# A decoder layer on one core: four units of the output projection and half the depth of an up-projection unit by a 7-product block scheme

## The chip, the core and the metric

The kernel runs on one core of one Trainium2 chip. The metric is the device time of one launch in microseconds (us). One execution was also taken with the hardware profiler; its rows give the start of each instruction, counted from the start of the span, on TensorE (PE, with its weight loads as PEld), VectorE (DVE), ScalarE (ACT), GpSimd (POOL) and SyncE (SP, which here only issues DMAs).

## What is computed

One layer on 256 tokens of width 2048 (16 chunks of 128), all in f32. Cut to what the change touches:

```python
mix = concat([conv_out, pool_out, att])      # 6 + 6 + 4 chunks of 128
x = x + mix @ w_out                          # 2048 x 2048
h = rmsnorm(x, g_ffn)
u = causal_dwconv(h @ w_up, ffn_conv_w) + ffn_conv_b   # w_up: 2048 x 2*5632
gate, val = split(u, 2)
x = x + (silu(gate) * val) @ w_down
return rmsnorm(x, g_final)
```

## The kernel before

**Precision.** Each f32 product is made of three matmuls in fp32r: both operands are split into a high part `hi` (a copy rounded to fp32r, by ACT) and a low part `lo = raw - hi` (by DVE), and hi·hi, hi·lo and lo·hi are summed in PSUM. The activations (`mixT`, `h2T`, `sums`) are split once, and are the stationary operand (128x128); the weights are split tile by tile as they come, and are the moving operand (128x512).

**The weight stream.** All weights are a list of tiles, `stream`, of 1 MB each (128 partitions x 2048 f32). `next_tile()` takes the next one, and first loads (SP issues the DMA into one of three `raw` buffers) and splits (`split_tile`, L131 on ACT and L132 on DVE) the tiles ahead of it. `raw`, `hi` and `lo` have three buffers each: the `hi` of a tile can start only when PE has ended the tile three places before it. This is the clock of ACT and DVE in all the stages of interest.

**Output projection** (two halves of the columns, 8 tiles each, loop over `n2` ahead of `add_in`). A tile is 2 chunks of depth by 1024 columns: 24 matmuls (`mm_b`, L436, L439, L442: 2 chunks x 2 token blocks x 2 column blocks x 3). The chunks come in the order 6 to 15, then 0 to 5 (`out_order`), since the conv chunks 0 to 5 are made last. After each half `add_in` (L804) adds the four banks of PSUM to `xt` and ACT squares them (L807). In the second half the first 8 chunks of the new x are transposed into `h2T` after tiles 3 and 4 of that half; the other 8 after the first tile of the up-projection.

**Up-projection** (`up`, L845). 11 units of 512 gate and 512 value columns; a unit has 8 tiles of 4 chunks x 512 columns, 24 matmuls each. When a half of a unit is complete, ACT scales it out of PSUM (`z`, L860), and in the middle of the next tile PE transposes it (`pz`, L871) for `up_finish`: the conv, silu and product (L879, L881, L885, L895), whose result goes to `u_raw`.

**Down-projection by blocks** (`turn`, `prod`, `Blocks`). For each pair of units the 1024 rows of `w_down` meet 256 tokens. Split 2 x 2 on depth and on columns (`b11`, `b12`, `b21`, `b22`, 1 MB each, in `ffn`), a 1024-column half is made by 7 products of 12 matmuls (`prod`, L947) where the plain form has 8 times 12. `turn` makes the four sums of the activation blocks (L916 to L918, L921, split by L922 and L925). The sums of the weight blocks are made by DVE (`add`, L245) and by DMAs that add to what is in the buffer, issued by POOL (`add_far`, L242). Each product is added to `xt` by DVE (L953). The 14 products of a pair stand between the up tiles of the next pair, one after each tile. For the first two units no such products are there yet.

**What sets the order.** The instructions of an engine run in the order in which they stand. The framework's scheduler sets it from the order of the code and its own priorities; SP's DMAs wait in one queue, so a load that waits for its buffer holds the loads behind it.

## Time and profile before

| | |
|---|---|
| median of 3 runs (lowest to highest) | 1044.55 us (1044.29 to 1045.07) |
| the profiled execution | 1044.61 us |
| its span, first to last instruction | 1042.7 us |
| DVE busy, ACT busy | 75%, 56% of the span |
| DMA | 220.77 MB, 212 GB/s over the span |
| granted TensorE clock | 0.997 |
| output projection, first and last PE matmul start | 228.4 us and 316.9 us |
| up-projection, first and last PE matmul start | 317.3 us and 983.5 us |

The profiled execution takes 1.9 us more than its span; what is worked out from rows is set against 1044.61 us. A row such as `x1408 | 448.8, 391 | 0.0` gives the count, the busy us, the mean ns of one and the idle us ahead of the group. Matmuls overlap, so the mean of one is longer than its share of the time: shares are read from the chain in order of time, which counts each stretch once.

### The profile page before, as it was taken

The numbers are of one execution on the slowest core, as the hardware profiler recorded it, in microseconds if no ns is written. First come the engines' busy times: TensorE is split into PE (matmuls) and PEld (weight loads), VectorE is DVE, ScalarE is ACT, GpSimd is POOL, SyncE is SP. The second block draws the span as 40 slices with busy tenths as digits, with TensorE's granted clock in tenths as the row PEclk, the third lists the DMA queues.
The fourth block names the chain that finished last, engine by engine and source line by source line (L and its number), as shares of the span: only waits on it lengthen the run. The fifth ranks groups of instructions, "written<-read, shape, count | busy, mean of one in ns | idle before, by whom it ended". The sixth has DMA issues, their size and how long they took to land.

```text
span 1042.7 us, 12612 instructions
## 1 busy us (share of the span) xinstructions
PE 1032.7 (99%) x4994; PEld 867.8 (83%) x4994; DVE 778.2 (75%) x833; ACT 586.7 (56%) x646; POOL 56.6 (5%) x93
## 2 busy tenths in 40 slices
PE   9999999999999999999999999999999999999996
PEld 8888888888888888888888888888888888888885
DVE  5677685764546566978879788797877978789776
ACT  6865354443446545665655655566556655665653
POOL 0013500000000000000000000000000000000000
PEclk9999999999999999999999999999999999999998
DMA  9665465555585464596976979768796687967932
GB/s 328 243 224 180 145 204 190 173 179 184 202 288 197 162 202 145 160 289 194 262 243 167 275 193 261 234 188 258 202 260 222 200 256 206 262 215 195 282 117 81
DMA packets 122020, 220.77 MB, mean 212 GB/s; under 512 B 3906, under 2 KB 35946, under 8 KB 121834
## 3 DMA queue, kind: packets, MB, share of 16 engines
q1 hardware_dynamic: 112426, 201.09, 57.1%
q0 software_dynamic: 9504, 18.88, 11.3%
q8 instruction: 39, 0.64, 0.2%
q14 instruction: 19, 0.16, 0.0%
q10 hardware_dynamic: 32, 0.01, 0.0%
HBM read 217.86 MB, written 2.10 MB: 211 GB/s over the span
## 4 chain that ended last, share of the span: by engine, by line
PE 98%; DVE 1%; ACT 0%; issue 0%; DVEq 0%
PE pu L845 46%; PE pp_a L947 9%; PE pp_b L947 5%; PE po L442 3%; PE po L439 3%; PE po L436 3%; PE pp_c L947 2%; PE pa_cb L403 2%; PE pa_pv L403 2%; PE pa_cx L403 2%; PE pa_cc L403 2%; PE pp L966 2%; PE pz L871 2%; PE pk L493 1%; PE pa_q L403 1%; PE pa_cb L407 1%
## 5 line engine op out<-in xcount | busy, mean ns | idle before, releaser
L845 PE MATMUL pu<-hi,h2T 128*128 128x512 f32 x1408 | 448.8, 391 | 0.0
L132 DVE TENSOR_TENSOR lo<-raw,hi 128x2048 fp32r<-128x2048 f32 (+3 forms) x156 | 333.0, 2136 | 137.8 <-ACT hi L131 137.2
L131 ACT ACTIVATE hi<-raw 128x2048 fp32r<-128x2048 f32 (+3 forms) x156 | 279.4, 1794 | 154.3 <-PE po L442 39.2
L845 PEld LDWEIGHTS pu<-hi,h2T 128*128 128x128 f32 x1408 | 264.4, 188 | 54.2
L845 PE MATMUL pu<-lo,h2T 128*128 128x512 f32 x704 | 274.6, 390 | 0.0
L253 DVE TENSOR_TENSOR lo<-ffn,hi 128x2048 fp32r<-128x2048 f32 x63 | 144.2, 2290 | 66.6 <-ACT hi L252 66.6
L252 ACT ACTIVATE hi<-ffn 128x2048 fp32r<-128x2048 f32 x63 | 120.7, 1917 | 98.0 <-PE pu L845 73.7
L845 PEld LDWEIGHTS pu<-lo,h2T 128*128 128x128 f32 x704 | 132.3, 188 | 27.5 <-DVE lo L132 0.7
L947 PE MATMUL pp_a<-hi,sums 128*128 128x512 f32 x288 | 94.5, 389 | 0.0
L881 DVE SCALAR_TENSOR_TENSOR t<-pz,cols,t 128x255 f32<-128x255 f32 (+1 forms) x176 | 79.5, 478 | 10.2 <-ACT t L879 9.2
L879 ACT ACTIVATE t<-pz,cols 128x256 f32<-128x256 f32 x88 | 46.9, 558 | 46.2 <-DVE t L881 24.1
L947 PEld LDWEIGHTS pp_a<-hi,sums 128*128 128x128 f32 x288 | 54.1, 188 | 11.2
L242 POOL DMA_DIRECT2D ffn<-in_w_down_dram x18 | 23.2, 1291 | 615.3 <-DVE ffn L245 494.3
L860 ACT ACTIVATE z<-pu,r_x 128x512 f32<-128x512 f32 x44 | 30.2, 687 | 46.7 <-PE pu L845 46.7
L947 PE MATMUL pp_a<-lo,sums 128*128 128x512 f32 x144 | 56.1, 389 | 0.0
L947 PE MATMUL pp_b<-hi,sums 128*128 128x512 f32 x144 | 47.3, 389 | 0.0
L245 DVE TENSOR_TENSOR ffn<-ffn 128x2048 f32<-128x2048 f32 x18 | 41.2, 2286 | 0.0
L436 PE MATMUL po<-hi,mixT 128*128 128x512 f32 x128 | 39.6, 391 | 0.0
L442 PE MATMUL po<-hi,mixT 128*128 128x512 f32 x128 | 39.5, 389 | 0.0
L439 PE MATMUL po<-lo,mixT 128*128 128x512 f32 x128 | 39.4, 389 | 0.0
L947 PEld LDWEIGHTS pp_a<-lo,sums 128*128 128x128 f32 x144 | 27.0, 188 | 5.6
L947 PEld LDWEIGHTS pp_b<-hi,sums 128*128 128x128 f32 x144 | 27.0, 188 | 5.6
(223 smaller groups left out, 1287.1 us busy)
## 6 DMA issues: line engine op xcount, KB each, us to landing
raw<-in_w_up_dram SPq DMA_DIRECT2D x88, 1024.0 KB, 7.3
ffn<-in_w_down_dram SPq DMA_DIRECT2D x40, 1024.0 KB, 6.2
raw<-in_w_in_dram SPq DMA_DIRECT2D x28, 1024.0 KB, 5.0
ffn<-in_w_down_dram POOLq DMA_DIRECT2D x18, 1024.0 KB, 10.4
raw<-in_w_out_dram SPq DMA_DIRECT2D x16, 1024.0 KB, 4.9
raw<-in_w_kv_dram SPq DMA_DIRECT2D x4, 1024.0 KB, 6.9
raw<-in_w_down_dram SPq DMA_DIRECT2D x4, 1024.0 KB, 5.2
raw<-in_w_kv_dram SPq DMA_DIRECT2D x6, 512.0 KB, 8.4
```

What stands on the lines that cost most here:

```text
L131: nc.scalar.activation(hi[:, s, :], raw[:, s, :], AF.Copy)
L132: nc.vector.tensor_tensor(lo[:, s, :], raw[:, s, :], hi[:, s, :].bitcast(F32), op=ALU.subtract)
L252: nc.scalar.activation(hi, raw, AF.Copy)
L253: nc.vector.tensor_tensor(lo, raw, hi.bitcast(F32), op=ALU.subtract)
L403: nc.tensor.matmul(ps[mi], hi[:, kk, c], actT[:, k, :], start=first and kk == 0, stop=False)
L436: nc.tensor.matmul(ps[tb][n], ah, hi[:, kk, c], start=f, stop=False)
L439: nc.tensor.matmul(ps[tb][n], ah, lo[:, kk, c], start=False, stop=False)
L442: nc.tensor.matmul(ps[tb][n], al, hi[:, kk, c], start=False, stop=l)
L845: nc.tensor.matmul(ps[tb], x_, y_[:, kk, :], start=k == 0 and n == 0, stop=k == KC - 1 and n == 2,)
L879: nc.scalar.activation(t, v, AF.Identity, bias=cvec("ffn_conv_b", m), scale=cw[2])
L881: nc.vector.scalar_tensor_tensor(t[:, s:], v[:, : S - s], cw[2 - s], t[:, s:], op0=ALU.mult, op1=ALU.add)
L947: nc.tensor.matmul(ps, a, b[:, j, :], start=first and j == 0 and n == 0, stop=j == 3 and n == 2, skip_group_check=True,)
```

## The change

Two more places use the 7-product scheme.

**Output projection.** Chunks 6 to 13 (8 chunks, "four units" of two) by the right 1024 columns are done by 7 products, `p0` to `p6`, in place of four tiles. The 12 tiles that stay are called `t0` to `t11` here: t0 to t7 are the first half, t8 to t11 the rest of the second. The order on PE is t0 t1 t2 t3 t4 p0 t5 p1 t6 p2 t7 p3 p4 t8 p5 t9 p6 t10 t11. The activation sums are made at the start of the stage from `mixT` (hi and lo are added again, L933, then `make_forms`, L887 to L899) and stored in the upper half of `h2T`; the blocks of `w_out` and the raw sums are in a new tile `outp`, which takes the buffer that `hT` had.

**Up-projection, unit 1.** Units 0 and 1 are run together. The tiles of unit 0 are called `u0` to `u7`. Unit 1 (gate and value columns together, 1024) is done for chunks 0 to 7 by 7 products, `m0` to `m6`, and for chunks 8 to 15 by four tiles, `v12`, `v13` (gate) and `v02`, `v03` (value), so called after the pair in `UP_ORDER`. The order is u0 to u4, m0, u5, m1, u6, m2, u7, m3, v12, v13, m4, v02, m5, v03, m6. Here the partial sums of several products share a bank, and what one result must not have of the bank's sum is copied out (`snaps`, L1037 to L1041) and taken off again when the half is scaled out (`z`, L1064 to L1068: three on DVE, one on ACT, where before all were on ACT).

The first blocks of `w_down`, which were loaded ahead of unit 0, are now loaded when unit 1's products are being split. In the code behind, `turn` calls `make_forms`, which has the same instructions.

```diff
@@ -202,10 +202,6 @@
     out_order = list(range(NCONV, KC)) + list(range(NCONV))
-    for n2 in range(2):
-        for k in out_order[::2]:
-            plan_b(w_out, k, 2, n2 * 1024, 1024, 2)
@@ -220,19 +216,25 @@
-        def __init__(self, seq, gi, p):
-            self.seq, self.gi, self.p = seq, gi, p
-            self.k0 = group_of[gi][0] * 4
+        def __init__(self, seq, gi, p, w=w_down):
+            self.seq, self.gi, self.p, self.w = seq, gi, p, w
+            self.k0 = NCONV if gi is None else group_of[gi][0] * 4
@@ -281,6 +283,35 @@
+    class OutBlocks(Blocks):
+        def buf(self, name):
+            return out_raw[:, {"b11": 0, "b22": 1, "b12": 2, "b21": 2}[name]]
+        def stationary(self, i, j):
+            if 1 <= i <= 4:
+                return out_form[:, i - 1, 0, j], out_form[:, i - 1, 1, j]
+            tb, s = {0: (0, 0), 5: (0, 1), 6: (1, 1)}[i]
+            k = NCONV + 2 * j + s
+            return tuple(mixT[:, k, h * S + tb * P : h * S + (tb + 1) * P] for h in range(2))
+    out_blocks = OutBlocks(0, None, 1, w_out)
+    out_sched = []
+    for n2 in range(2):
+        pairs = out_order[::2] if n2 == 0 else out_order[8::2]
+        for i, k in enumerate(pairs):
+            out_sched.append((n2, k, i == 0, i == len(pairs) - 1))
+            n_after = ((0, 0, 0, 0, 1, 1, 1, 2), (1, 1, 0, 0))[n2][i]
+            for _ in range(n_after):
+                out_sched.append(("prod", sum(o[0] == "prod" for o in out_sched)))
+    for o in out_sched:
+        if o[0] == "prod":
+            stream.append((out_blocks, None, o[1], 1))
+        else:
+            plan_b(w_out, o[1], 2, o[0] * 1024, 1024, 2)
@@ -294,6 +325,31 @@
+    class UpBlocks(Blocks):
+        U = 1
+        def source(self, name):
+            s, h = int(name[1]) - 1, int(name[2]) - 1
+            c0 = (1 - h) * D_UP + self.U * 512
+            src = w_up[: 8 * P, c0 : c0 + 512]
...
+    up_blocks = UpBlocks(2, None, 0)
+    up_blocks.next = blocks[0]
+    UP_ORDER = [0, 1, 2, 3, 4, ("m", 0), 5, ("m", 1), 6, ("m", 2), 7, ("m", 3), ("m", (1, 2))]
+    UP_ORDER += [("m", o) for o in ((1, 3), 4, (0, 2), 5, (0, 3), 6)]
@@ -307,6 +363,11 @@
         for t in range(n_t):
+            if gi == 0:
+                if t == 0:
+                    for o in UP_ORDER:
+                        sched.append(("up", 0, o) if isinstance(o, int) else ("mixed", UpBlocks.U, o[1]))
+                continue
             sched.append(("up", a + t // 8, t % 8))
             for _ in range(after[t]):
                 sched.append(prods.pop(0))
@@ -319,6 +380,10 @@
+        elif what == "mixed" and isinstance(b, int):
+            stream.append((up_blocks, None, b, 1))
+        elif what == "mixed":
+            plan_b(w_up, 4 * b[1], 4, (1 - b[0]) * D_UP + a * 512, 512, 4)
         else:
             stream.append((a, None, b, 1))
@@ -809,21 +874,92 @@
-    for n2 in range(2):
-        ps = [[bank(f"po_{n2}_{tb}_{n}") for n in range(2)] for tb in range(TB)]
-        for i in range(KC // 2):
-            mm_b(ps, next_tile(), mixT, out_order[2 * i : 2 * i + 2], range(TB), i == 0, i == KC // 2 - 1)
-            if n2 == 1 and i in (2, 3):
-                transpose_in(xt, h2T, "g_ffn", range((i - 2) * 4, (i - 1) * 4), "x2")
-        add_in(ps, n2 * 2, range(TB), f"o{n2}", ssq4)
+    def make_forms(raw, form, four, own, nm, t=None):
+        v = raw.rearrange("p (j s) (b t) -> p s b j t", s=2, b=TB)
+        a11, a12, a21, a22 = v[:, 0, 0], v[:, 1, 0], v[:, 0, 1], v[:, 1, 1]
+        if t is None:
+            t = wpool.tile([P, 4, 4, P], F32, tag="raw", name=f"turn_{nm}")
...
+        tt(t[:, 0], a21, a22, op=ALU.subtract)
+        tt(t[:, 2], a11, a21, op=ALU.subtract)
+        tt(t[:, 1], t[:, 0], a11, op=ALU.subtract)
+        tt(t[:, 3], t[:, 1], a12, op=ALU.add)
+        nc.scalar.activation(four(0), t, AF.Copy)
+        tt(four(1), t, four(0).bitcast(F32), op=ALU.subtract)
+    outp = apool.tile([P, 4, 2048], F32, tag="act", name="outp")
+    out_raw = outp[:, :3, :].rearrange("p i (j c) -> p i j c", c=512)
+    mix_raw = outp[:, 3, :].rearrange("p (c t) -> p c t", t=S)
+    mix_8 = mixT[:, NCONV : NCONV + 8, :].bitcast(F32)
+    nc.vector.tensor_tensor(mix_raw, mix_8[:, :, :S], mix_8[:, :, S:], op=ALU.add)
+    out_form = h2T[:, 8:, :].rearrange("p (f s) (j t) -> p f s j t", s=2, t=P)
+    make_forms(
+        mix_raw, None, lambda half: out_form[:, :, half], (), "mix",
+        out_blocks.buf("b12").rearrange("p j (f t) -> p j f t", t=P),
+    )
+    at_tile = 0
...
+        n2, k, first, last = o
+        if first:
+            ps = [[bank(f"po_{n2}_{tb}_{n}") for n in range(2)] for tb in range(TB)]
+            at_tile = 0
+        mm_b(ps, next_tile(), mixT, (k, k + 1), range(TB), first, last)
+        at_tile += 1
+        if n2 == 0 and at_tile <= 3:
+            out_blocks.load(("b11", "b22", "b12")[at_tile - 1])
+        if n2 == 1 and at_tile in (2, 3):
+            transpose_in(xt, h2T, "g_ffn", range((at_tile - 2) * 4, (at_tile - 1) * 4), "x2")
+        if last:
+            add_in(ps, n2 * 2, range(TB), f"o{n2}", ssq4)
-    for name in ("b11", "b22", "b12"):
-        blocks[0].load(name)
@@ -852,12 +988,84 @@
+        if u == 0 and b == 1:
+            h2_8 = h2T[:, :8, :].bitcast(F32)
+            nc.vector.tensor_tensor(u_raw, h2_8[:, :, :S], h2_8[:, :, S:], op=ALU.add)
+            make_forms(
+                u_raw, None, lambda half: sums[:, 1:5, half], (), "h2",
+                up_blocks.buf("b12").rearrange("p j (f t) -> p j f t", t=P),
+            )
+            for name in ("b11", "b22", "b12"):
+                up_blocks.load(name)
+        todo.append(lambda: up_finish(u, w, z))
+    def up_mixed(u, what):
+        hi, lo = next_tile()
+        r = r_2[0]
+        snaps = [u_raw[:, 4 + 2 * i : 6 + 2 * i, :].rearrange("p c t -> p (c t)") for i in range(2)]
+        if what == 1:
+            up_ps["snap"] = wpool.tile([P, 512], F32, tag="raw", name="snap")
+        snaps.append(up_ps.get("snap"))
...
+        if isinstance(what, int):
+            chain, first = (("a", 1), ("b", 1), ("a", 0), ("a", 0), ("b", 0), ("c", 0), ("a", 0))[what]
+            ps = mm(
+                chain, [up_blocks.stationary(what, j) for j in range(4)], bool(first), what != 5
+            )
+            if what in (0, 2):
+                nc.scalar.activation(snaps[what // 2], ps, AF.Copy, scale=r[:, 0:1])
+            elif what == 1:
+                nc.scalar.activation(snaps[2], ps, AF.Copy, scale=r[:, 1:2])
+            elif what == 3:
+                nc.vector.scalar_tensor_tensor(
+                    snaps[2], ps, r[:, 1:2], snaps[2], op0=ALU.mult, op1=ALU.subtract
...
+                chain = ("c", "a")[tb] if not right else ("b", "d")[tb]
+                mm(chain, pairs, q == 2 and chain in "cd", q == 3)
...
+        z = [spool.tile([P, 512], F32, tag="w2k", name=f"z_{u}_{w}_{tb}") for tb in range(TB)]
+        stt = nc.vector.scalar_tensor_tensor
+        if w == 0:
+            stt(z[0], up_ps["b"], r[:, 0:1], snaps[1], op0=ALU.mult, op1=ALU.subtract)
+            stt(z[1], up_ps["d"], r[:, 1:2], snaps[2], op0=ALU.mult, op1=ALU.subtract)
+        else:
+            stt(z[0], up_ps["c"], r[:, 0:1], snaps[0], op0=ALU.mult, op1=ALU.add)
+            nc.scalar.activation(z[1], up_ps["a"], AF.Copy, scale=r[:, 1:2])
         todo.append(lambda: up_finish(u, w, z))
@@ -1072,7 +1233,7 @@
     for what, a, b in sched:
-        {"up": up, "prod": prod, "plain": plain}[what](a, b)
+        {"up": up, "mixed": up_mixed, "prod": prod, "plain": plain}[what](a, b)
```

How the built programs differ at the three places that the prediction speaks of. Line numbers of the changed kernel are its own.

The first place is DVE at the end of the input projection and the start of the output projection. Before, the queue reads as follows; lo_2217, lo_2284 and lo_2314 are the low parts of the second, third and fourth tile of `w_out` (t1, t2 and t3 in the names above):

```order
L132 TENSOR_TENSOR lo_2217<-raw_2176,hi_2216 128x2048
L778 SCALAR_TENSOR_TENSOR cv_2160<-cu_2154,cols,cv_2160 128x256
L778 SCALAR_TENSOR_TENSOR cv_2170<-cu_2164,cols,cv_2170 128x256
L778 SCALAR_TENSOR_TENSOR cv_2160<-cu_2154,cols,cv_2160 128x256
L778 SCALAR_TENSOR_TENSOR cv_2170<-cu_2164,cols,cv_2170 128x256
L132 TENSOR_TENSOR lo_2284<-raw_2214,hi_2283 128x2048
L537 TENSOR_TENSOR mixT<-pat_2252,mixT 128x256
L421 TENSOR_TENSOR cb_2261<-pa_cb_0_2174,cb_2261 128x256
L421 TENSOR_TENSOR cb_2268<-pa_cb_1_2175,cb_2268 128x256
L422 TENSOR_TENSOR cb_2261<-cb_2261,row_x 128x256
```

After, at the same place, lo_2217 is again t1's (t2's, lo_2292, stands two rows behind the end of this piece):

```order
L933 TENSOR_TENSOR outp<-mixT 128x2048
L602 TENSOR_TENSOR mixT<-pat_2252,mixT 128x256
L486 TENSOR_TENSOR cb_2261<-pa_cb_0_2174,cb_2261 128x256
L486 TENSOR_TENSOR cb_2268<-pa_cb_1_2175,cb_2268 128x256
L487 TENSOR_TENSOR cb_2261<-cb_2261,row_x 128x256
L487 TENSOR_TENSOR cb_2268<-cb_2268,row_x 128x256
L855 TENSOR_TENSOR cb_2261<-cb_2261,cv_2160 128x256
L855 TENSOR_TENSOR cb_2268<-cb_2268,cv_2170 128x256
L890 TENSOR_TENSOR outp<-outp 128x512
L602 TENSOR_TENSOR mixT<-cb_2261,mixT 128x256
L602 TENSOR_TENSOR mixT<-cb_2268,mixT 128x256
L891 TENSOR_TENSOR outp<-outp 128x512
```

The rebuilding of the raw activations (L933) stands where t2's low part stood, the three small sums stand between the conv's last steps, and t2's low part is behind all of them.

The second place is DVE and SP in the up-projection's first tiles. Before, on DVE, from the last transposes into `h2T` on, the low parts of u3, u4, u5 and u6 follow each other:

```order
L346 SCALAR_TENSOR_TENSOR h2T<-pt_x_12_2880,cols,h2T 128x256 x2
L346 SCALAR_TENSOR_TENSOR h2T<-pt_x_14_2889,cols,h2T 128x256 x2
L132 TENSOR_TENSOR lo_2913<-raw_2832,hi_2912 128x2048
L132 TENSOR_TENSOR lo_2945<-raw_2910,hi_2944 128x2048
L132 TENSOR_TENSOR lo_2975<-raw_2942,hi_2974 128x2048
L132 TENSOR_TENSOR lo_3005<-raw_2972,hi_3004 128x2048
```

After, lo_2928 and lo_2968 are u3's and u4's, lo_2998 is m0's and lo_3028 is u5's:

```order
L411 SCALAR_TENSOR_TENSOR h2T<-pt_x_14_2904,cols,h2T 128x256 x2
L132 TENSOR_TENSOR lo_2928<-raw_2847,hi_2927 128x2048
L891 TENSOR_TENSOR ffn<-ffn 128x512
L892 TENSOR_TENSOR ffn<-ffn 128x512
L895 TENSOR_TENSOR ffn<-ffn 128x512
L132 TENSOR_TENSOR lo_2968<-raw_2925,hi_2967 128x2048
L899 TENSOR_TENSOR sums<-ffn,sums 128x4x512
L255 TENSOR_TENSOR lo_2998<-ffn,hi_2997 128x2048
L247 TENSOR_TENSOR ffn<-ffn 128x2048
L132 TENSOR_TENSOR lo_3028<-raw_2995,hi_3027 128x2048
```

On SP, after, raw_2995, raw_3055 and raw_3108 are the loads of u5, u6 and u7, and the next row is the load of block b12 of `w_up` (the loads of b11 and b22 stand further ahead); before, loads of up tiles follow each other here:

```order
L120 DMA raw_2995<-in_w_up_dram 128x4x512
L120 DMA raw_3055<-in_w_up_dram 128x4x512
L120 DMA raw_3108<-in_w_up_dram 128x4x512
L241 DMA ffn<-in_w_up_dram 128x4x512
L120 DMA raw_3187<-in_w_up_dram 128x4x512
```

Block b12's buffer holds the raw sums until L899 has read them, so its load comes after L899; DVE's add of b12 to b11 (L247) waits for that load, and u5's low part (lo_3028) stands right behind the add.

The third place is DVE where the first half of unit 1 is scaled out. Before, that is ACT's work (ACT's queue, L860, the gate half of unit 1):

```order
L131 ACTIVATE hi_3254<-raw_3222 128x2048
L131 ACTIVATE hi_3284<-raw_3252 128x2048
L860 ACTIVATE z_0_0_3312<-pu_0_0_3160,r_x_2901 128x512
L860 ACTIVATE z_0_1_3314<-pu_0_1_3161,r_x_2901 128x512
L131 ACTIVATE hi_3320<-raw_3282 128x2048
L879 ACTIVATE t_0_0_3346<-pz_0_0_3336,cols 128x256
```

After, on DVE, lo_3322 is v02's low part, lo_3352 is m5's and lo_3373 is v03's:

```order
L132 TENSOR_TENSOR lo_3322<-raw_3259,hi_3321 128x2048
L1089 SCALAR_TENSOR_TENSOR t_1_3_3300<-pz_1_2_3283,cols,t_1_3_3300 128x255
L1089 SCALAR_TENSOR_TENSOR t_1_3_3300<-pz_1_2_3283,cols,t_1_3_3300 128x254
L1103 TENSOR_TENSOR ffn<-t_0_3_3170,t_1_3_3300 128x256
L255 TENSOR_TENSOR lo_3352<-ffn,hi_3351 128x2048
L1064 SCALAR_TENSOR_TENSOR z_0_0_3368<-pm_b,r_x_2916,ffn 128x512
L1065 SCALAR_TENSOR_TENSOR z_0_1_3369<-pm_d,r_x_2916,snap 128x512
L132 TENSOR_TENSOR lo_3373<-raw_3349,hi_3372 128x2048
L1089 SCALAR_TENSOR_TENSOR t_0_0_3399<-pz_0_0_3389,cols,t_0_0_3399 128x255
L1089 SCALAR_TENSOR_TENSOR t_0_0_3399<-pz_0_0_3389,cols,t_0_0_3399 128x254
```

The two scalings (L1064, L1065) have moved from ACT to DVE, and stand behind m5's low part.

More of the change, by code (lines that the diff above doesn't have):

```diff
@@ new lines, with prod @@
+    chains = {}
+    def prod(bl, i):
+        hi, lo = next_tile()
+        chain, first, tb, right, op = (
+            ("a", True, 0, 0, ALU.add),
+            ("b", True, 1, 1, ALU.add),
+            ("a", False, 0, 1, ALU.subtract),
+            ("a", False, 1, 1, ALU.subtract),
+            ("b", False, 0, 1, ALU.add),
+            ("c", True, 0, 0, ALU.add),
+            ("a", False, 1, 0, ALU.add),
+        )[i]
+        if first:
+            chains[chain] = bank(f"pp_{bl.gi}_{bl.p}_{chain}")
+        ps = chains[chain]
+        for j in range(4):
+            ah, al = bl.stationary(i, j)
+            for n, (a, b) in enumerate(((ah, hi), (ah, lo), (al, hi))):
+                nc.tensor.matmul(
+                    ps, a, b[:, j, :], start=first and j == 0 and n == 0,
+                    stop=j == 3 and n == 2, skip_group_check=True,
+                )
+        c0 = bl.p * 1024 + right * 512
+        o = xt[:, tb, c0 : c0 + 512]
+        nc.vector.tensor_tensor(o, o, ps, op=op)
```

105 lines of the change are left out of this document (58 added, 47 removed).

## The prediction

> **What bounds the kernel now.** The page's first part and its chain of waits (shares of the span) come first, then the chain in order of time (start, us, what):
>
> ```profile
> PE 1032.7 (99%) x4994; PEld 867.8 (83%) x4994; DVE 778.2 (75%) x833; ACT 586.7 (56%) x646; POOL 56.6 (5%) x93
> PE 98%; DVE 1%; ACT 0%; issue 0%; DVEq 0%
> ```
> ```profile
> 317.43 5.45 PE pu L845 x24
> 322.88 1.75 PE pt_x L334 x16
> 354.57 0.87 PE pz L871 x8
> 431.60 2.72 PE pp_a L947 x12
> 443.39 5.44 PE pu L845 x24
> ```
>
> The path to the end is TensorE's row of matmuls, one behind the other. A tile of 24 takes 5.44 us, a product of 12 takes 2.72: 0.2267 us each. What an engine beside PE does counts only where PE waits for it. The view of the up-projection's line shows how seldom it does (us, times):
>
> ```profile
>   DVE lo L132: 0.7, 3
> ```
>
> So the question is in two parts: what leaves PE's row, and where the added work of DVE, ACT and the DMAs comes too late.
>
> **What leaves the row.** Output projection: four tiles (96 matmuls) become seven products (84). Unit 1's first 8 chunks: the same, 96 to 84. Transposes stay as many. That is 24 matmuls x 0.2267 = **5.44 us**, 2.72 in each place. How one matmul is priced is a choice; the groups by line give two other figures for it (busy us, mean ns of one, idle ahead):
>
> ```profile
> L845 PE MATMUL pu<-hi,h2T 128*128 128x512 f32 x1408 | 448.8, 391 | 0.0
> L845 PEld LDWEIGHTS pu<-hi,h2T 128*128 128x128 f32 x1408 | 264.4, 188 | 54.2
> ```
>
> 391 ns is the length of one with its overlap; 24 of these would make 9.4 us, and the tile takes 5.44, so it is no price. 188 ns is its weight load, with 54.2 us of idle time between the loads: loads are not back to back. I take the tile's 0.2267. The Trainium skill, "Perfetto Trace Analysis", section "Identifying the Most-Contended Engine", says that matmul busy time is no measure of how close TensorE is to its limit, and that the share of weight loads is to be used. On the first the trace agrees (391 ns against 227). By the second the 24 would be worth their weight loads, 24 x 0.188 = 4.51 us, an estimate; the tile of 24 taking 5.44 us, not 4.51, speaks against it.
>
> **What is added to DVE and ACT, in sum.** The windows (us, then busy and count of PE, PEld, DVE, ACT, POOL; clock; DMA share; GB/s) of the output projection, of units 0 and 1, and of a stage that has the 7-product scheme already:
>
> ```profile
> 228.40:316.90 88.50, 88.50 (x401) 73.47 (x400) 45.94 (x39) 36.75 (x37) 0.00 (x0) 1.00 0.64 224
> 317.40:405.00 87.60, 87.60 (x409) 73.06 (x408) 50.94 (x56) 49.66 (x61) 0.96 (x5) 1.00 0.56 185
> 430.00:560.00 130.00, 130.00 (x592) 107.97 (x591) 107.87 (x97) 76.31 (x68) 6.00 (x5) 1.00 0.78 227
> ```
>
> The durations of what is added are there, since later stages run the same forms. In order of time on DVE, a large sum, an addition to xt and an add of two blocks; then the group rows of a small sum and of the only scaling from PSUM with 512 columns:
>
> ```profile
> 429.71 2.29 DVE L925 TENSOR_TENSOR sums<-turn,sums 128x2048 fp32r<-128x2048 f32 x1
> 431.91 2.29 DVE L132 TENSOR_TENSOR lo<-raw,hi 128x2048 fp32r<-128x2048 f32 x1
> ...
> 436.38 0.68 DVE L953 TENSOR_TENSOR xt<-xt,pp_a 128x512 f32<-128x512 f32 x1
> 436.97 2.29 DVE L245 TENSOR_TENSOR ffn<-ffn 128x2048 f32<-128x2048 f32 x1
> 439.18 2.28 DVE L132 TENSOR_TENSOR lo<-raw,hi 128x2048 fp32r<-128x2048 f32 x1
> ```
> ```profile
> L917 DVE TENSOR_TENSOR turn<-ffn x5: 678/685/686, 420.2 to 936.4; 128x512 f32<-128x512 f32 x5
> L578 DVE SCALAR_TENSOR_TENSOR misc<-pv,r_mem,misc x2: 730/735/740, 71.5 to 72.1; 128x512 fp32r<-128x512 f32 x2
> ```
>
> From start to start a 128x2048 takes 2.21 us (429.71 to 431.91), a 128x512 0.59, a scaling about 0.65. The output projection gets 3 more low parts (19 tiles for 16), two block adds, L933 and L899 (8 x 2.21 = 17.7), 4 small sums (2.4) and 7 additions to xt (4.1): 24.2, hence 70 of 85.8 us, 82%. Units 0 and 1 get the same without the seven additions, and four scalings: 50.9 + 17.7 + 2.4 + 2.6 = 73.6 of 84.9, 87%. The stage at 430 has 83% with PE busy all of its 130 us. So DVE stays below PE; the small excess over the known 83% is a reason to follow the queue where it is tight. ACT gets four copies (about 1.9 each) and stays under 60 us. No cost can be below nothing here: PE is busy all of both windows, so there is no idle time to win. Each block scheme also loads 6 MB for 4: some 2 MB more in each stage, to about 250 GB/s, against a stage that had 227 with the same scheme.
>
> **Where it is tight: three places of DVE's queue, and one more.** The clock of hi and lo is read from ACT and DVE (start, us, engine, line; in brackets idle time and what ended it), beside PE's first matmul of the stage:
>
> ```profile
> 227.45 0.40 PE L407 MATMUL pa_cb<-hT,lo 128*128 128x256 f32 x2
> 228.41 0.63 PE L436 MATMUL po<-hi,mixT 128*128 128x512 f32 x2
> ```
> ```profile
> 245.00 1.92 ACT L131 ACTIVATE hi<-raw 128x2048 fp32r<-128x2048 f32 x1 [3.52 <-PE po L442]
> ```
> ```profile
> 226.24 1.66 DVE L778 SCALAR_TENSOR_TENSOR cv<-cu,cols,cv 128x256 f32<-128x256 f32 x4
> 232.20 0.75 DVE L421 TENSOR_TENSOR cb<-pa_cb,cb 128x256 f32<-128x256 f32 x2
> 232.86 0.75 DVE L422 TENSOR_TENSOR cb<-cb,row_x 128x256 f32<-128x256 f32 x2
> 246.95 2.29 DVE L132 TENSOR_TENSOR lo<-raw,hi 128x2048 fp32r<-128x2048 f32 x1 [3.15 <-ACT hi L131]
> 298.98 1.65 DVE L346 SCALAR_TENSOR_TENSOR h2T<-pt_x,cols,h2T 128x256 fp32r<-128x256 f32 x4
> 324.23 3.23 DVE L346 SCALAR_TENSOR_TENSOR h2T<-pt_x,cols,h2T 128x256 fp32r<-128x256 f32 x8 [1.25 <-PE pt_x L334]
> ```
>
> The third tile ends at 228.41 + 3 x 5.44 = 244.73; its buffer's next hi starts 0.27 later, the low part 1.95 behind and is done 2.21 on: 4.43 us from buffer to split tile.
>
> *Start of the output projection.* L933 writes into hT's old buffer, which PE reads until about 227.8; DVE is busy to 227.9 anyway. Behind it stand 2.2 (L933), 7 steps of 256 columns (two take 0.66, so 2.35), a small sum (0.6), 2 such steps (0.7), two sums (1.2) and t2's low part (2.2): done at 237.1 to 237.6. PE wants t2 at 228.41 + 10.88 = 239.29. Margin 1.7 or more; cost 0. Even twice the price for L933 would cost 0.5.
>
> *From t7 to t8.* t8's hi waits for t7's end, t8's low part is ready 4.43 after it, and p3 and p4 keep PE for 5.44. Margin 1.0; cost 0.
>
> *Block b12 of unit 1.* Up tiles now start 2.72 earlier, at 314.71. u1's low part waits for t10's buffers (6.3 before that), so it ends at 312.8; the four steps of the last transposes (1.65) and `add_in` (2.4) end at 316.9. Then come u2's low part, L993, a small sum, the eight steps (3.2), u3's low part, three small sums, u4's low part and L899: 2.2 x 5 + 0.6 x 4 + 3.2 + some 0.5 for the rstd = 17.1, to 334.0. Only then can b12's load be issued. The loads of such blocks (view of their line, 280 to 560 us; then the page's rows of issues, median us to landing last):
>
> ```profile
> DMA to landing us min/median/max: 6.0/6.2/9.9
> ```
> ```profile
> ffn<-in_w_down_dram SPq DMA_DIRECT2D x40, 1024.0 KB, 6.2
> ffn<-in_w_down_dram POOLq DMA_DIRECT2D x18, 1024.0 KB, 10.4
> ```
>
> With 6.2 it lands at 340.2, the add ends at 342.4, u5's low part at 344.6. PE wants u5 after u0 (5.45), the transposes (1.75), u1 to u4 (21.76) and m0 (2.72): 346.39. Margin 1.8, less about 0.5 for hand-overs: a landing of up to some 7.5 us costs nothing. At 9.9 it costs 2.4, at POOL's 10.4 2.9. I take 0, since the load of u7 is the only one right ahead of it; bounds 0 to 2.9. Behind the waiting add stand the low parts of u5 and m1, and PE waits for them. The loads that add (POOL) have about 9 us to spare: b12's sum is needed only for p3 and m3.
>
> *Scaling of unit 1's gate half.* Say m4 ends at T. m5's hi waits for v13's buffer, free at T - 2.72; its low part runs from T - 0.5 to T + 1.7. The two scalings stand behind it: T + 2.35 and T + 3.0. PE transposes both in the middle of v02, the second from T + 2.83. It waits **about 0.3 us**. Before, ACT did this. Bounds: 0, if the scalings run as fast as an addition to xt, to 0.9, if the low part is another 0.6 late. m6's half has one scaling on each engine and a whole tile of time: 0.
>
> **The sum.** 1044.61 - 5.44 + 0.3 = 1039.5 us. The profiled execution (1044.61) stands 0.06 over the median of the runs (1044.55), which is less than their spread of 0.8; no correction.
>
> **Rivals.**
>
> *Block b12 comes late* (chance 13%). For it: b12 is behind L899 in a queue that I followed by hand over 17 us, and one of the eleven loads of its kind took 9.9 us. Against: the median of 6.2 with two adding DMAs about. Price 1 to 2.9 us: 1040.5 to 1042.4; most of this is still faster.
>
> *Many small waits* (6%): each of the 14 new products waits 0.15 to 0.3 us, as the three waits of 0.7 in all show that margins near 0 do exist. 2.1 to 4.2 us: 1041.6 to 1043.7. Against: the products from 430 to 560 stand in the same alternation, and PE is busy all of that window.
>
> *A matmul is worth its weight load* (3%): 1044.61 - 4.51 + 0.3 = 1040.4. This is the skill's rule above.
>
> *DVE becomes the bound: slower than before* (7%). If the new operations, which read mixT and h2T in strided pieces and write into the halves of h2T and sums, cost a multiple, DVE's sum passes PE's. In the output projection this begins where the added 24.2 become 39.9 (1.65 times), and the layer is slower than before by 0.2% from about 47 us on, or, with both stages over, from some 43.5 and 37.6. From there it is 1046.7 and more; between the two points the time is about that of before. Against: L917 and L925 read and write such pieces already, at 0.59 and 2.21 from start to start.
>
> That the work isn't removed is no rival: the order of PE holds 24 matmuls fewer.
>
> **How the numbers follow.** The forecast has 71%, and by itself 1038.8 (the lowest run of before less 5.44, and no wait) to 1040.4. The range reaches into the first two rivals, **1038.7 to 1042.0**; beyond it lie the end of the late landing, most of the small waits, and DVE as the bound. A measurement of this kernel can tell 0.2%, 2.1 us, from no change: faster means under 1042.46, slower over 1046.6. Faster: 71 for the forecast, 12 of the 13 for b12, 2 of the 6 for small waits, 3 for the weight loads, 88 in all. Same: 1 of b12, 4 of the small waits, 2 of DVE as the bound, 7. Slower: the other 5 of DVE.
>
> **What would show it.** PE should have 24 matmuls fewer, and the chain should be all but PE. Out of the projection: PE's first up matmul at 314.7 instead of 317.4; if later, the missing part has its row among PE's waits, for t2, t8 or a product. In units 0 and 1: a wait of pz for DVE's z of 0.2 to 0.4 us at some 389 us; none at u5 near 346; if there is one, DVE's L247 should show idle time that ended with a DMA. First product of w_down at about 426.5 (431.6 before). I am wrong if PE's row has idle time over 1 us in all between 228 and 430, or if a matmul in the new tiles starts at another spacing than 0.227 us.

## The result, and the profile after

| | median of runs (lowest to highest) | ratio to before, 95% interval |
|---|---|---|
| before | 1044.59 us (1044.29 to 1045.07) | |
| after | 1039.19 us (1038.98 to 1039.66) | 0.9948 [0.9936, 0.996] |

The kernel became 5.40 us faster, within the forecast's own range and 0.3 us under its 1039.5. The profiled execution took 1039.66 us, with a span of 1037.9.

The page of the changed kernel, busy times and shares of the chain:

```profile
PE 1026.7 (99%) x4970; PEld 861.9 (83%) x4970; DVE 820.5 (79%) x866; ACT 601.8 (58%) x654; POOL 64.1 (6%) x97
PE 98%; DMA 1%; DVE 0%; SPq 0%; DVEq 0%; issue 0%; ACT 0%
```

PE has 24 matmuls fewer (4994 to 4970), and is still what bounds the kernel; DVE went from 75% to 79%. The view of PE's waits between 228 and 430 us has no row, before or after. The chain in order of time (start, us, what) of the changed kernel gives the stages; in front of it stands the first matmul of the output projection, from the timeline:

```profile
228.90 0.63 PE L501 MATMUL po<-hi,mixT 128*128 128x512 f32 x2
```
```profile
315.20 5.45 PE pu L981 x24
...
344.17 2.72 PE pm_a L1024 x12
346.89 5.44 PE pu L981 x24
...
386.77 2.73 PE pm_c L1024 x12
389.50 0.22 PE pz L1079 x2
389.72 0.24 PE pm_a L1024
389.96 0.67 PE pz L1079 x6
390.63 2.51 PE pm_a L1024 x11
...
426.68 2.72 PE pp_a L921 x12
```

In this execution the output projection began 0.49 us later than in the one of before (228.90 to 228.41), ahead of anything that was changed; so lengths are compared, not times of day.

| stretch | before | after | difference |
|---|---|---|---|
| t0 to u0 | 317.43 - 228.41 = 89.02 | 315.20 - 228.90 = 86.30 | -2.72 |
| u0 to the first product of `w_down` | 431.60 - 317.43 = 114.17 | 426.68 - 315.20 = 111.48 | -2.69 |

Each place gave back its 12 matmuls (2.72), and all waits together cost 0.03 us. A new product takes 2.72 like the old ones. The windows of the two stretches (us, then busy of PE, PEld, DVE, ACT, POOL):

```profile
228.40:314.00 85.60, 85.60 (x390) 71.14 (x389) 66.12 (x54) 44.78 (x41) 2.74 (x2) 1.00 0.77 245
314.70:399.00 84.30, 84.30 (x394) 70.23 (x393) 69.41 (x71) 56.27 (x64) 5.87 (x7) 1.00 0.70 210
```

DVE is at 77% and 82%, PE is busy all of both, and the DMAs move 245 and 210 GB/s.

### The profile page after: what moved, and what is told of

Its sections match the earlier page's. It is cut to its first block, busy times and chain, and to the rows that moved or that the text cites. A ratio compares the mean times of both kernels' runs of the same rounds, so it can differ in the third digit from the quotient of the medians.

```text
span 1037.9 us, 12624 instructions
## 1 busy us (share of the span) xinstructions
PE 1026.7 (99%) x4970; PEld 861.9 (83%) x4970; DVE 820.5 (79%) x866; ACT 601.8 (58%) x654; POOL 64.1 (6%) x97
## 4 chain that ended last, share of the span: by engine, by line
PE 98%; DMA 1%; DVE 0%; SPq 0%; DVEq 0%; issue 0%; ACT 0%
PE pu L981 42%; PE pp_a L921 9%; PE pp_b L921 5%; PE pp_c L921 2%; PE pa_cb L468 2%; PE pa_pv L468 2%; PE pa_cx L468 2%; PE pa_cc L468 2%; PE po L504 2%; PE pp L1127 2%; PE po L501 2%; PE po L507 2%; PE pz L1079 2%; PE pm_a L1024 2%; PE pa_q L468 1%; PE pk L558 1%
## 5 line engine op out<-in xcount | busy, mean ns | idle before, releaser
L981 PE MATMUL pu<-hi,h2T 128*128 128x512 f32 x1280 | 409.4, 391 | 0.0
L132 DVE TENSOR_TENSOR lo<-raw,hi 128x2048 fp32r<-128x2048 f32 (+3 forms) x148 | 314.7, 2128 | 70.9 <-ACT hi L131 69.9
L131 ACT ACTIVATE hi<-raw 128x2048 fp32r<-128x2048 f32 (+3 forms) x148 | 264.3, 1789 | 110.5 <-issue 34.7
L981 PEld LDWEIGHTS pu<-hi,h2T 128*128 128x128 f32 x1280 | 240.3, 188 | 49.4
L981 PE MATMUL pu<-lo,h2T 128*128 128x512 f32 x640 | 249.5, 390 | 0.0
L255 DVE TENSOR_TENSOR lo<-ffn,hi 128x2048 fp32r<-128x2048 f32 x70 | 160.3, 2290 | 72.0 <-ACT hi L254 72.0
L254 ACT ACTIVATE hi<-ffn 128x2048 fp32r<-128x2048 f32 x70 | 134.0, 1916 | 105.1 <-PE pu L981 75.0
L1087 ACT ACTIVATE t<-pz,cols 128x256 f32<-128x256 f32 x88 | 46.9, 558 | 48.1 <-DVE t L1089 24.2
L247 DVE TENSOR_TENSOR ffn<-ffn 128x2048 f32<-128x2048 f32 x20 | 45.7, 2287 | 3.4 <-DMA ffn<-in_w_up_dram 3.4
L468 PE MATMUL pa_cb<-hT,hi 128*128 128x512 f32 x96 | 30.7, 400 | 0.0
L468 PE MATMUL pa_pv<-hT,hi 128*128 128x512 f32 x96 | 30.2, 396 | 0.0
L468 PE MATMUL pa_cc<-hT,hi 128*128 128x512 f32 x96 | 30.2, 395 | 0.0
```

The costliest lines, as they stand in the source:

```text
L131: nc.scalar.activation(hi[:, s, :], raw[:, s, :], AF.Copy)
L132: nc.vector.tensor_tensor(lo[:, s, :], raw[:, s, :], hi[:, s, :].bitcast(F32), op=ALU.subtract)
L247: nc.vector.tensor_tensor(self.buf(to), self.buf(to), self.buf(what), op=ALU.add)
L254: nc.scalar.activation(hi, raw, AF.Copy)
L255: nc.vector.tensor_tensor(lo, raw, hi.bitcast(F32), op=ALU.subtract)
L468: nc.tensor.matmul(ps[mi], hi[:, kk, c], actT[:, k, :], start=first and kk == 0, stop=False)
```

## The experiments

The theory: the gain is 24 x 0.2267 us out of PE's row, the parts add up, and all else is hidden by margins of about 1 us. Against it stand a price by weight loads, and an end that something else sets (a late block, DVE). Each edit is made in the changed kernel, and each time is set against its 1039.19 us and, as a ratio, against runs of before on the same chip. Line numbers move by a few between kernels.

### The two halves apart

*Output projection alone*: units 0 and 1 in their old order, `forms` and the loads of their blocks left out, the loads of `w_down` ahead of unit 0 again.

```diff
-            if gi == 0:
-                if t == 0:
-                    for o in UP_ORDER:
...
-        if u == 0 and b == 1:
...
+    for name in ("b11", "b22", "b12"):
+        blocks[0].load(name)
```

> Only the output projection has the block scheme; units 0 and 1 of the up-projection are as before. If TensorE's row is the bound and each of the 12 matmuls that leave it is worth 0.2267 us: 2.72 us less than before, 1041.9 us, with PE's first up matmul 2.72 us earlier after the start of the projection than before, and no wait of PE in that stage. If a matmul is worth its weight load of 188 ns: 2.26 less, 1042.3. If the whole gain comes from the up-projection: no change, 1044.6. If the gain of the full change were more than its parts (DVE relieved elsewhere), less than 2 us here.

*Units 0 and 1 alone*: the output projection as before.

```diff
-        pairs = out_order[::2] if n2 == 0 else out_order[8::2]
+        pairs = out_order[::2]
...
+            n_after = 0
...
-    make_forms(
-        mix_raw, None, lambda half: out_form[:, :, half], (), "mix",
...
```

> Only unit 1's first 8 chunks have the block scheme; the output projection is as before. TensorE's row as the bound: 2.72 us less than before, 1041.9 us, so that the two halves add up to the full change's 5.4. By weight loads: 1042.3. If the new waits (block b12, the scalings on DVE) cost here what was left open (0.3 and up to 2.9 us), 1042.2 to 1044.8.

Measured: 1041.94 us (0.9976 [0.9967, 0.9986]) and 1041.88 us (0.9973 [0.9962, 0.9983]), each against its 1044.61. That is -2.67 and -2.73; their sum, -5.40, is what both did together. The chains of the two, first u0, then the first product of `w_down`:

```profile
316.47 5.45 PE pu L978 x24
...
430.65 2.72 PE pp_a L916 x12
```
```profile
317.10 5.45 PE pu L968 x24
...
428.61 2.72 PE pp_a L921 x12
```

From u0 to the first product it is 114.18 us with the old units (114.17 before) and 111.51 with the new (111.48 after). The profiled execution of the first kernel took 1043.55 us, 1.6 more than its median, and began the projection late, at 230.17 us; from there to u0 it is 86.30, the length of the changed kernel. The 5.4 us come from these two places, half each, and neither costs the other anything.

### What a matmul is worth

The seven products of the output projection with each matmul cut into two of 256 columns: the same columns through PE, twice the weight loads in 84 matmuls.

```diff
+            parts = (slice(0, 256), slice(256, 512)) if bl is out_blocks else (slice(0, 512),)
...
-                nc.tensor.matmul(ps, a, b[:, j, :], ...)
+                for c in parts:
+                    nc.tensor.matmul(ps[:, c], a, b[:, j, c], ...)
```

> In the seven products of the output projection each matmul of 512 columns is made as two of 256, so 24 matmuls and 24 weight loads a product in place of 12; the same sums. If a matmul costs its columns (256-column matmuls of the input projection start 0.12 us apart): a product takes 24 x 0.12 = 2.88 for 2.72 us, 7 of them 1.1 us more than the changed kernel, some 1040.3. If the weight load of 0.188 us is what paces TensorE: 24 x 0.188 = 4.5 us a product, 12.5 us more, 1051.7.

Measured: 1040.42 us (0.9961 [0.9946, 0.9977]), +1.2. In the chain of this kernel, a product of 24 halves, and in its groups by line, their weight loads (busy us, mean ns of one, idle ahead):

```profile
263.86 2.87 PE pp_None_b L923 x24
```
```profile
L923 PEld LDWEIGHTS pp_None_b<-hi,h2T 128*128 128x128 f32 x32 | 4.6, 192 | 0.1
```

The product takes 2.87 us in place of 2.72, so a half starts every 0.12 us, while one weight load is 0.192 us long: loads overlap, and the mean length of a load is no price any more than that of a matmul is. Seven products at 0.15 more are 1.05 of the 1.2 us. The Trainium skill, "Perfetto Trace Analysis", section "Identifying the Most-Contended Engine", takes the share of weight loads, beside the share of the peak FLOPs, as what tells how near TensorE is to its limit. That a matmul is worth its weight load was the prediction's reading of it, and is not borne out here: 84 loads more cost 1.2 us, and 24 matmuls fewer saved 5.40.

### A block that comes late

The load of b12 of unit 1 is issued twice, so that the block lands some 5 us later.

```diff
-            for name in ("b11", "b22", "b12"):
+            for name in ("b11", "b22", "b12", "b12"):
                 up_blocks.load(name)
```

> Block b12 of unit 1 is loaded twice, the second load into the same place behind the first, so that its sum waits for the second. In the profile of the changed kernel the load lands 5.5 us after its issue, DVE's add waits 3.4 us for it, and u5's low part is ready at 345.75, 1.1 us before PE wants it. If that margin is what hides the wait: the second load lands 2.5 to 5.5 us later, and the kernel takes 1.4 to 4.4 us more than the changed one, 1040.6 to 1043.6, with PE waiting for u5's low part. If the wait of DVE is off the path whatever its length: 1039.2, no change.

Measured: 1040.17 us (0.9954 [0.9941, 0.9968]), +1.0: less than the theory of the margin gives (1.4 to 4.4). DVE's timeline (start, us; in brackets the idle time ahead and what ended it) of the changed kernel, then of this one, shows why:

```profile
335.59 2.28 DVE L255 TENSOR_TENSOR lo<-ffn,hi 128x2048 fp32r<-128x2048 f32 x1
341.25 2.29 DVE L247 TENSOR_TENSOR ffn<-ffn 128x2048 f32<-128x2048 f32 x1 [3.38 <-DMA ffn<-in_w_up_dram]
343.46 2.29 DVE L132 TENSOR_TENSOR lo<-raw,hi 128x2048 fp32r<-128x2048 f32 x1
```
```profile
335.12 2.28 DVE L255 TENSOR_TENSOR lo<-ffn,hi 128x2048 fp32r<-128x2048 f32 x1
340.30 2.29 DVE L132 TENSOR_TENSOR lo<-raw,hi 128x2048 fp32r<-128x2048 f32 x1 [2.90 <-ACT hi L131]
345.73 2.29 DVE L247 TENSOR_TENSOR ffn<-ffn 128x2048 f32<-128x2048 f32 x1 [3.14 <-DMA ffn<-in_w_up_dram]
```

In the changed kernel u5's low part (L132) stands behind the add that waits for b12 (L247). With the second load the scheduler put it ahead of the add: PE had u5 in time, and waited at m1 (0.33 us, for its low part); the transposes of z and the matmul between them took 0.35 us more than in the changed kernel (z0 and z1 were ready 0.33 us later behind the end of m4). So this run priced another order, and not the one that was forecast.

The next kernel keeps the order: b12 is loaded twice, and a small subtraction that reads the sum and writes into u5's low part stands between add and low part. A second one has the subtraction, and one load.

```diff
+                state["pin"] = self if isinstance(self, UpBlocks) else None   # in split(), behind self.add("b11", "b12")
...
+        if state.get("pin") is not None:
+            b11 = state["pin"].buf("b11")[:, 0, :256]
+            nc.vector.tensor_tensor(lo[:, 0, :256], b11, b11, op=ALU.subtract)
         nc.vector.tensor_tensor(lo[:, s, :], raw[:, s, :], hi[:, s, :].bitcast(F32), op=ALU.subtract)
```

> As in the run with b12's load issued twice, so the block lands some 5 us later than in the changed kernel (345.6 instead of 341.2), but here a subtraction of 128x256 that reads the sum and writes into u5's low part keeps u5's low part behind the waiting add on DVE, as it stands in the changed kernel; in the run without it u5's low part stood ahead of the add. If it is the place behind the waiting add that prices a late block, u5's low part is ready at about 348.0 + 0.3 + 2.2 = 350.5 where PE wants it at 346.9 to 347.1, so PE waits 3.4 to 3.7 us at u5: 1042.3 to 1043.2. If the order doesn't matter, 1040.2 as without it. If a late block costs nothing, 1039.2.

> The changed kernel with only the subtraction of 128x256 between the add for b12 and u5's low part, and b12 loaded once. It puts u5's low part 0.3 to 0.5 us later, where the changed kernel has a margin of 1.1 us: 1039.2 if that margin is there; 1039.5 or more if it isn't.

Measured: with one load 1039.17 us (0.9945 [0.9929, 0.9962]), no change, so the margin at u5 is there. The subtraction puts u5's low part 0.7 us later: it starts 2.92 us behind the start of the add, where it is 2.21 in the changed kernel. With two loads 1045.27 us (1.0007 [0.9997, 1.0016]): 6.1 more, as slow as before the change, and beyond the 1042.3 to 1043.2 expected. Its profile is of the fastest of its ten executions, 1044.40 us. PE's waits (us in total, times, longest) are about what was expected, 3.3 us for 3.4 to 3.7:

```profile
PE pm_b L1029 <- ACT hi L258: 2.9, 1, 2.9
PE pu L986 <- DVE lo L136: 0.4, 1, 0.4
```

They cost more than their length. The chain of this kernel, and its windows ahead of, in and behind that place (the number before the DMA share is the granted clock):

```profile
350.78 6.63 PE pu L986 x22
...
431.56 2.72 PE pp_a L926 x12
```
```profile
345.00:350.70 5.70, 2.44 (x10) 1.47 (x8) 4.99 (x4) 3.48 (x3) 1.30 (x1) 0.96 0.07 6
350.70:353.70 3.00, 2.92 (x7) 2.37 (x8) 3.00 (x3) 0.92 (x1) 0.00 (x0) 0.50 1.07 188
353.70:358.00 4.30, 4.30 (x21) 3.54 (x20) 3.63 (x2) 1.24 (x2) 0.00 (x0) 1.00 0.97 228
```

After the wait the granted clock is 0.50 for 3 us: 22 matmuls take 6.63 us where they need 22 x 0.2267 = 4.99, 1.64 more. Whether the clock falls because PE stood idle, or something else beside it (the DMAs start again then), is told by filling the wait: 14 matmuls into the bank of m1, which m1 overwrites.

```diff
+        if u == 0 and b == 5:
+            up_ps["b"] = bank("pm_b")
+            for _ in range(14):
+                nc.tensor.matmul(up_ps["b"], h2T[:, 0, :P], hi[:, 0, :], start=True, stop=True)
...
-            if first:
+            if first and what != 1:
                 up_ps[chain] = bank(f"pm_{chain}")
```

> As the run with b12 loaded twice and u5's low part kept behind the add, with 14 more matmuls on PE (128x512, from u5's high part into the bank of m1, which m1 overwrites), which stand right behind m0, ahead of u5. That run's profile has 3.35 us of waits of PE at u5 and m1, then a granted clock of 0.50 from 350.8 to 353.7, where a matmul takes 0.43 us in place of 0.227. The 14 take 14 x 0.2267 = 3.17 us of the wait's 3.35. If the lower clock follows from PE's idle time, it is gone here: first product of w_down about 1.6 us earlier than the 431.56 of that run, so 1042.5 to 1043.1 us. If it is something else in that stretch (the DMAs, the engines beside), 1044.4 to 1045.3 as there. If the 14 come on top, 1047.6 to 1048.5.

Measured: 1043.74 us (0.9992 [0.9982, 1.0001]), 1.5 less than without the 14, though more work is done. The chain and a window of this kernel:

```profile
351.14 5.28 PE pu L990 x22
...
430.57 2.72 PE pp_a L926 x12
```
```profile
351.10:354.10 3.00, 2.96 (x13) 2.46 (x14) 3.00 (x2) 1.02 (x2) 0.00 (x0) 1.00 1.03 173
```

The clock stays at 1.00 with the DMAs as busy (1.03), and the same 22 matmuls take 5.28 us. So the clock fell for PE's idle time. The time is 0.6 over the range expected. In part the loads did that: the two of b12 took 10.58 us in place of 10.12, the add started at 345.88 in place of 345.52, and u5 came as much later (0.36). The 22 matmuls took 0.29 more than the 4.99.

### The scaling on DVE

z1, the second scaling of unit 1's gate half, is done twice.

```diff
-            stt(z[1], up_ps["d"], r[:, 1:2], snaps[2], op0=ALU.mult, op1=ALU.subtract)
+            for _ in range(2):
+                stt(z[1], up_ps["d"], r[:, 1:2], snaps[2], op0=ALU.mult, op1=ALU.subtract)
```

> The scaling of the second token block of unit 1's gate half is done twice on DVE, so that z1 is ready 0.65 us later than the 389.6 of the changed kernel. If PE's order (two transposes of z0, a matmul of v02, then the transposes of z1 from 389.96) leaves a slack of 0.34 us, PE's pz waits 0.3 us in its row and the time is 1039.5. If the forecast's wait of 0.3 us is there already, unseen, the wait grows by all of the 0.65: 1039.85, and the stretch of 6.37 us (v02 and the transposes) becomes 7.0.

Measured: 1039.14 us (0.9945 [0.9931, 0.996]), no change, and neither theory. DVE's timeline and the chain of this kernel:

```profile
388.60 0.74 DVE L1066 SCALAR_TENSOR_TENSOR z<-pm_d,r_x,snap 128x512 f32<-128x512 f32 x1
389.26 2.28 DVE L132 TENSOR_TENSOR lo<-raw,hi 128x2048 fp32r<-128x2048 f32 x1
391.46 0.75 DVE L1066 SCALAR_TENSOR_TENSOR z<-pm_d,r_x,snap 128x512 f32<-128x512 f32 x1
```
```profile
389.14 0.22 PE pz L1080 x2
389.36 2.75 PE pm_a L1024 x12
392.11 0.46 PE pm_c L1024 x2
392.57 0.66 PE pz L1080 x6
```

The scheduler put a low part between the two scalings, and on PE moved the other six transposes 14 matmuls back, where z1 is ready. So z1 came 2.5 us later and not 0.65, and the slack that was to be tested was not. A transpose is not bound to "the middle of the tile"; that it stands where the scheduler reckons that its operand will be there fits both orders, and was not tested by itself.

### DVE until it is the bound

The low part of each of the 14 new products is made twice, then three times, by DVE.

```diff
+            for _ in range(2 if isinstance(self, (OutBlocks, UpBlocks)) else 1):      # then 3
                 nc.vector.tensor_tensor(lo, raw, hi.bitcast(F32), op=ALU.subtract)
```

> Each of the 14 new products gets a second, equal low part on DVE (2.21 us more each, the same result written twice). DVE's work then is 66.1 + 15.5 = 81.6 of 85.6 us in the output projection and 69.4 + 15.5 = 84.9 of 84.3 us in units 0 and 1. If DVE is the next bound, as its sums say: little in the projection, and waits of PE for low parts in units 0 and 1; 2 to 8 us more than the changed kernel, 1041 to 1047. If DVE has the room that its share of 79% over the span suggests: no change, 1039.2.

> Two more equal low parts for each new product. DVE's work is 97.1 for 85.6 us and 100.4 for 84.3 us: over by 11.5 and 16.1. If DVE is the bound from there on: at least 27.6 us more than the changed kernel, 1067 to 1078, slower than before. If waits come only where DVE's queue is tight: under 15 us more.

Measured: 1046.93 us (1.0021 [1.0012, 1.003]) with one more, +7.7, and 1078.05 us (one run) with two more, +38.9. Windows of the first of these, and the row of ACT in the last of them:

```profile
228.40:314.00 85.60, 82.49 (x369) 67.27 (x368) 77.70 (x57) 42.37 (x37) 2.74 (x2) 1.00 0.70 217
...
255.00:260.00 5.00, 5.00 (x24) 4.14 (x23) 3.27 (x2) 3.28 (x2) 1.11 (x1) 1.00 0.60 84
...
285.00:290.00 5.00, 3.09 (x13) 2.18 (x12) 5.00 (x5) 1.46 (x1) 0.00 (x0) 1.00 0.52 197
```
```profile
288.54 1.91 ACT L254 ACTIVATE hi<-outp 128x2048 fp32r<-128x2048 f32 x1 [3.74 <-DMA outp<-in_w_out_dram]
```

DVE's sum is 77.7 of 85.6 us (91%) and PE loses time all the same: 4.2 us from t0 to u0, where little was expected, and 3.2 from u0 to the first product of `w_down`. Where products and additions come close together (285 to 290) DVE has no gap and PE is idle for 1.9 of 5 us; at 255 DVE has 1.7 us to spare that it can't use for them. Of the 1.9 us, 1.2 are a wait for p4's second low part. The other 0.7 begin a wait for p5's hi, and that one waits for the load of b21, which is issued only when p3's second low part is done (280.72 us; 276.9 in the changed kernel). The reserve is in each place, not in the sum. One thing is not told apart: the second low part also lengthens the way of each new product to PE by 2.2 us, more than the margins of about 1 us, and no run added work on DVE that nothing waits for.

With two more, 17.1 us are lost from t0 to u0 and 21.8 from u0 to the first product, where DVE's sums are over PE's by 11.5 and 16.1. So there DVE's sum gives the larger part; the granted clock was 0.94 and 0.96 in the two windows, and the rest stays open.

### The seven products in a row

The products of the output projection stand one behind the other after t7, in place of between the tiles.

```diff
-            n_after = ((0, 0, 0, 0, 1, 1, 1, 2), (1, 1, 0, 0))[n2][i]
+            n_after = ((0, 0, 0, 0, 0, 0, 0, 7), (0, 0, 0, 0))[n2][i]
```

> The seven products of the output projection stand one behind the other after t7, in place of one after each tile; the same work. PE needs 19.0 us for them; DVE needs 7 low parts, two adds of blocks and seven additions to xt, 24 us, and a hi buffer comes free only every 2.72 us. If the alternation of tiles and products is what hides DVE's work: PE waits 5 us or more among the products, 1044 to 1050, the gain of this place and more is lost. If the order of the work doesn't matter as long as DVE's sum is below PE's: 1039.2.

Measured: 1050.84 us (1.0056 [1.0039, 1.0072]), +11.65; the same matmuls, and slower than before the change. PE's waits of this kernel, two windows of it, and a row of ACT:

```profile
PE pp_None_b L921 <- DVE lo L255: 2.2, 1, 2.2
PE pp_None_a L921 <- DVE lo L255: 1.6, 1, 1.6
PE pp_None_c L921 <- ACT hi L254: 1.4, 1, 1.4
PE pp_None_a L921 <- ACT hi L254: 1.3, 1, 1.3
```
```profile
285.00:290.00 5.00, 4.69 (x14) 3.76 (x15) 0.85 (x2) 0.00 (x0) 0.00 (x0) 0.66 1.09 272
...
295.00:300.00 5.00, 4.47 (x13) 3.44 (x14) 5.00 (x4) 2.27 (x2) 0.00 (x0) 0.66 0.15 20
```
```profile
291.76 3.71 ACT L254 ACTIVATE hi<-outp 128x2048 fp32r<-128x2048 f32 x2 [9.23 <-DMA outp<-in_w_out_dram]
```

A product keeps PE for 2.72 us, half of a tile, but takes a whole tile's hi and low part, and some an add or a load before that; a plain tile between two products is what gives ACT, DVE and the loads their time. The waits are 6.5 us. The last two of them (1.4 and 1.3, for the hi of p5 and p6) are the price of a load: b21 takes the buffer of b12, so it is issued when p3's low part is done (283.08 us), and ACT waits 9.23 us for it. The rest of the 11.65, which made it more than expected, is for the larger part the clock again: 0.66 in two windows of 5 us loses about 1.7 us in each. Some 1.8 us stay open.

## Why the prediction was right, and where it was not

**What leaves the row** (-5.44): right in size and place, -2.72 and -2.69 in the trace, -2.67 and -2.73 alone. The choice of 0.2267 us, the tile's share, for a matmul was right; the weight load's 0.188 was not, as the run with split columns shows.

**What is hidden** (0 at the start, at t8 and at b12): right, PE waits for none of them. t2's low part was done at 237.7 for 239.8 (forecast: margin of 1.7 or more), t8's at 285.2 for 286.0 (forecast 1.0). At b12 the queue followed by hand was 1.2 us late where L899 ends (335.7 for 334.0, of which 0.49 is the later start), the landing took 5.5 us for 6.2, and u5's low part was done at 345.75 for 346.89: 1.1 us of margin where 1.3 to 1.8 was forecast. That it came so close is in part luck, as the late queue and the early landing go against each other.

**The price beyond that margin** was wrong. The prediction had 2.4 us for a landing of 9.9, 2.9 for one of 10.4. With the order kept and the block in place after 10.1 us PE's first product of `w_down` came 5.35 us later in the profiled execution (431.56 for 426.21 with one load), and the median was 6.1 over the changed kernel's. Of PE's waits of 3.3 us, 0.4 are for u5's low part, which the experiment's own subtraction made 0.7 later; the 2.9 that are left are near the 2.6 that the forecast has for a landing of 10.1. What was missed is behind the wait: PE's next 3 us ran at half the clock, 1.64 more. So this rival reached to about 1043.8 (an estimate: 1039.2, 2.9 and 1.64; the clock's part without the second, short wait was not measured), and by the median, which is 0.9 over the profiled execution, some 0.9 further, and not to 1042.4; the range's upper end was drawn too low for it. That it didn't occur doesn't make its price right.

**The wait for the two scalings** (+0.3) is the term that was mis-sized: it is 0.06 at most (v02 and its transposes take 6.37 us where 24 x 0.2267 and 0.87 are 6.31), and nearly all of the 0.3 us between forecast and result. The step took z1 to be wanted at T + 2.83, with both transposed in one go. In the changed kernel's chain, above, two transposes of z0 come first (389.50), then a matmul of v02, then the others (389.96). DVE's timeline has the scalings ahead of both:

```profile
388.30 0.74 DVE L1064 SCALAR_TENSOR_TENSOR z<-pm_b,r_x,ffn 128x512 f32<-128x512 f32 x1
388.96 0.74 DVE L1065 SCALAR_TENSOR_TENSOR z<-pm_d,r_x,snap 128x512 f32<-128x512 f32 x1
```

z0 is ready at about 389.0 and z1 at 389.7, 2.3 and 2.9 behind the end of m4 (386.77), as forecast; the time at which PE wants them was what failed. The room is small: in the run with b12's load issued twice they were 0.33 us later, and the same stretch took 0.35 us more. The order of PE is made by the scheduler, and the run with z1 twice shows that it moves the transposes when z1 is later.

**DVE's sums** were 66.1 and 69.4 us for 70 and 73.6: too high, half of it by a miscount: three low parts, two adds, the rebuilding (L933 or L993) and L899 are seven large operations in each stage, and the sum has eight (2.21 too much; by the same rows 22.0 are added in the projection and not 24.2). What was also wrong is the point from which DVE decides: 39.9 us added in the output projection, taken from the sum. With 37.5 (22.0 and seven low parts at 2.21) the stage t0 to u0 had already lost 4.2 us (318.95 - 228.44 = 90.51 for 86.30), though there the added work stands on the products' own way to PE. The 7% for this rival rested on a wider margin than there is; that it stayed out was right, since none of the new forms cost more than its row of before.

**Many small waits**: no row of PE's waits in either place. The alternation of tiles and products carries this, as the run with seven in a row shows.

## What to carry to other kernels

Price what leaves a bound engine's row by its share in the chain, and look for the reserve of the engines that feed it at each place of the row, not in their sums. When you price a wait of PE, add what the clock loses after it, and when you forecast a wait from the order of a queue, ask whether the scheduler would leave that order if the operand came later. A scheme with fewer matmuls per loaded block is to be spread between tiles that need less of the other engines.

## What the hardware showed that was not expected

A wait of PE of 2.9 us was followed by 3 us at a granted clock of 0.50, so 3.3 us of waits cost 5.0 in the row, and in most of the runs more (median 1045.27, lowest 1044.40); with 14 matmuls in the wait the clock stayed at 1.00. In the row of seven products a wait of 2.2 us was enough (the second window below), and two of 1.4 and 1.3 with one matmul between them (the third); after the wait of 1.6 the clock stayed (the first):

```profile
279.70:280.70 1.00, 1.00 (x4) 0.85 (x5) 0.54 (x1) 1.00 (x2) 0.74 (x1) 1.00 0.00 0
286.30:287.30 1.00, 1.00 (x4) 0.78 (x3) 0.00 (x0) 0.00 (x0) 0.00 (x0) 0.50 1.08 229
296.50:297.50 1.00, 1.00 (x4) 0.71 (x4) 1.00 (x1) 0.77 (x1) 0.00 (x0) 0.50 0.00 0
```

The Trainium skill, "TensorE: Matmul & The Clock Gate", section "Why this matters for your kernels", asks for no idle gaps above about 3 us, and gives a clock of 4/8 as what follows them. With the 4/8 the 0.50 of these runs agrees; but the wait of 2.2 us, after which the clock halved all the same, is shorter than 3. Whether it is the single gap that counts or the idle time of a longer stretch is not told by these runs.
